# Expert input features regrouped so that each transposing product reads 128 neighbouring columns

## Chip, cores and metric

One core of one Trainium2 chip. The metric is device time in microseconds of one launch; lower is better.

## What is computed

One decoder layer on 512 tokens of 1024 features, in float32: RMSNorm, one projection, three token mixers (a state space model, a pooling, a block-sparse attention), an output projection and a residual, then a mixture of experts, and a last RMSNorm. The change touches only the input side of the experts:

```python
h = rms_norm(x, norm2_g[l])
# hier_moe: top-1 of 4 groups, then top-2 of its 4 experts; comb holds the weights
hg = jnp.einsum('td,edf->tef', t, w_gate)     # 16 experts, d = 1024, f = 256
hu = jnp.einsum('td,edf->tef', t, w_up)
act = jax.nn.silu(hg) * hu * comb[..., None]
y = jnp.einsum('tef,efd->td', act, w_down)
```

The sum over d may be taken in any order of the features, as long as a token's row and the rows of `w_gate` and `w_up` use the same one.

## The kernel before

The kernel is one stream of instructions per engine. A planner (`Flow`, lines 104 to 278) runs many small generators (`s_...`), estimates when each step could start, and so fixes the order in which every engine gets its instructions; on the chip each engine then works through its own list in that order and waits on semaphores. All instructions of the planner's part carry line 96, so groups of the profile are told apart by tile names.

The mixture of experts works on slots, not on tokens. Each of the 16 experts has 96 slots (`CAPACITY`), so 1536 slots, cut into 12 units of 128 slots. Routing (`s_route`, once for each of four blocks of 128 tokens, m = 0 to 3) computes logits (`pl`, from the transposed rows `h2T`), finds the two best experts (`hot`), counts places with a product against a triangle (`pc`), and gets each token's slot (`slot_i`). Then a token's scaled row (`xs_m[m]`: tiles `xp` for m = 0 to 2, tile `xs` for m = 3) goes two ways:

- Unit 0 does not go through memory. `s_gather` (lines 1414 to 1430) multiplies the rows of block m by a 0/1 matrix `sel` (128 tokens by 128 slots) and adds up over the four blocks in two PSUM banks `gb`. A block takes eight products, k = 0 to 7, each with 128 of the 1024 features as the stationary operand (loaded into the array by a weight load) and `sel` as the moving one. Products of float32 leave two records each in the trace, so a block shows 16 and all four 64.
- Units 1 to 11 are written to a scratch tensor by scatters (GpSimd, indirect DMA), read back (`xr`, one load per unit, issued by SyncE in `s_xt`), and transposed on TensorE in `unit_xt` (lines 1595 to 1606): eight transposes into `tx` per unit, again with 128 features of each row as the stationary operand and the identity (`cpk`) moving. One record each, 88 in all.

In both, product k reads the features k, k+8, k+16, ...: the row is seen as `(c k)`, so neighbouring columns of the stationary operand lie 8 float32 apart. This fits how the experts' first matrices are loaded: `source` (line 1618) puts rows 8p to 8p+7 of a matrix in partition p, as one stretch of memory, so that the k-th row of every partition is again k, k+8, ...

After the gather or the transposes, ScalarE casts to float16 (`xts`, the high part), VectorE makes the low part, and `s_gate_up` runs the unit's products `pg` (24 steps), then `s_down` the activation, two transposes `pta` and the products `py`. Expert weights stream through five staging tiles (`st_lde`), and each is split into two float16 parts by ScalarE and VectorE (`gu`, `dn`). A branch for the case that an expert gets more than 96 tokens (`tc.If(rv > CAP)`, line 1907) has its own copy of the expert code in float32, with a third use of `(c k)` at line 1923.

Of the kernel before, what the change touches and what calls it, by code (L numbers as in the profile page):

```python
# [19 lines left out]
P = 128  # L20
D = 1024
S = 512
KD = D // P
# [15 lines left out]
NE = 16  # L39
FE = 256  # L40
# [240 lines left out]
def hybrid_trunk_kernel(tc, a, out, cap=CAPACITY, dbg=None):  # L281
# [22 lines left out]
    v, act, pe, pool, sp = fl.v, fl.act, fl.pe, fl.pool, fl.sp  # L304
# [36 lines left out]
    ident = cpk[:, C_ID:C_ID + P]  # L341
# [23 lines left out]
    def bank(tag, name):  # L365
        return psum[HALF[tag]].tile([P, 512], F32, tag=tag, name=name, bufs=BANKS[tag])
# [888 lines left out]
    def s_route(m):  # L1255
# [96 lines left out]
        for i, (e, _, _) in enumerate(owners(0)):  # L1352
            if i == 0:
                v.tensor_scalar(sel, cpk[:, C_COL:C_COL + P], pl_c[:, e:e + 1], None, ALU.is_equal)
            else:
                v.scalar_tensor_tensor(sel, cpk[:, C_COL:C_COL + P], pl_c[:, e:e + 1], sel, ALU.is_equal, ALU.add)
        fl.sig(("sel", m))
        fl.spawn(1, s_gather(m))
        if m == NT - 1:
            fl.spawn(0, s_count())  # L1360
# [23 lines left out]
    xs_m = {}  # L1384
# [12 lines left out]
    def parts_out(u, h, ps, end):  # L1397

        yield "act"
        hi, lo = (xT_[u][:, i * KD + 4 * h:i * KD + 4 * h + 4, :] for i in range(2))  # L1400
        src = ps.rearrange("p (k n) -> p k n", k=4)
        act.copy(hi, src)
        yield "dve"
        v.tensor_tensor(lo, src, hi, ALU.subtract)
        end()

    def unit_end(u, h, tag, left):
        def end():
            fl.give(tag)
            left[0] -= 1  # L1410
            if not left[0]:
                fl.sig(("xT", u))
        return end

    def s_gather(m):

        yield "pe", ((("sel", m - 1), ("gather", 0, m - 1)) if m else (("wo_end", 1),)) + (("xs", m),), () if m else ("mm", "mm")
        if m == 0:
            M["gb"] = [bank("mm", f"gb{i}") for i in range(2)]
        src = xs_m[m].rearrange("p (c k) -> p k c", k=KD)  # L1420
        for k in range(KD):
            if k == 4:
                yield "pe"
            pe.matmul(M["gb"][k // 4][:, (k % 4) * P:(k % 4 + 1) * P], src[:, k], M["sel"][:, m, 0],
                      start=(m == 0 and k % 4 == 0), stop=(m == NT - 1 and k % 4 == 3))
        fl.sig(("gather", 0, m))
        if m == NT - 1:
            xT_[0] = xts[0]
            left = [2]
            for h in range(2):  # L1430
                fl.spawn(0, parts_out(0, h, M["gb"][h], unit_end(0, h, "mm", left)))

    def unit_in(u):
        return xts[u % NXT]
# [159 lines left out]

    def unit_xt(u, xr):
        left = [2]
        src = xr.rearrange("p (c k) -> p k c", k=KD)
        for h in range(2):
            yield "pe", ("B", ("xr", u)), ("tx1",) if h else ("tx0", "xT")
            if h == 0:  # L1600
                xT_[u] = unit_in(u)
            tx = psum[h].tile([P, 512], F32, tag=f"tx{h}", name=f"tx{u}_{h}")
            for k in range(4):
                pe.transpose(tx[:, k * P:(k + 1) * P], src[:, 4 * h + k], ident)
            fl.spawn(0, parts_out(u, h, tx, unit_end(u, h, f"tx{h}", left)))
        fl.give("xr")
# [287 lines left out]
    v, act, pe, pool, sp = nc.vector, nc.scalar, nc.tensor, nc.gpsimd, nc.sync  # L1894

    def rstd(pl, src, name, junk):
        ss = pl.tile([P, 1], F32, name="ss" + name)
        act.activation(junk, src, AF.Square, accum_out=ss)
        ms = pl.tile([P, 1], F32, name="ms" + name)
        pool.tensor_scalar(ms, ss, 1.0 / D, EPS, ALU.mult, ALU.add)  # L1900
        rs = pl.tile([P, 1], F32, name="rs" + name)
        pool.tensor_tensor(rs, ms, nhalf, ALU.pow)
        return rs
# [3 lines left out]
    with tc.If(rv > CAP):  # L1907
        with tc.tile_pool(name="fb", bufs=1) as fb, tc.tile_pool(name="psF", bufs=2, space=PSUM) as psF:
            sp.dma_start(cov_scr, cov)
            gff = fb.tile([P, D], F32, name="gff")  # L1910
            sp.dma_start(gff, a["final_norm_g"].to_broadcast([P, D]))
            g2f = fb.tile([P, D], F32, name="g2f")
            sp.dma_start(g2f, a["norm2_g"].to_broadcast([P, D]))
            xtf = [fb.tile([P, D], F32, name=f"xtf{t}") for t in range(NT)]
            hTf = fb.tile([P, KD, S], F32, name="hTf")
            hs = fb.tile([P, D], F32, name="hs")
            for t in range(NT):
                sp.dma_start(xtf[t], x2_scr[t * P:(t + 1) * P, :])
                rs = rstd(fb, xtf[t], f"h{t}", hs.bitcast(F16)[:, 0:D])
                v.scalar_tensor_tensor(hs, xtf[t], rs, g2f, ALU.mult, ALU.mult)  # L1920
                for k in range(KD):
                    pt = psF.tile([P, 512], F32, tag="pf", name=f"pf{t}_{k}")
                    pe.transpose(pt[:, 0:P], hs.rearrange("p (c k) -> p k c", k=KD)[:, k], ident)
                    v.tensor_copy(hTf[:, k, t * P:(t + 1) * P], pt[:, 0:P])
            for t in range(NT):
                for i in range(2):
                    yf = fb.tile([P, D], F32, tag="yf", name=f"yf{t}_{i}")
                    sp.dma_start(yf, y_scr[i * S + t * P:i * S + (t + 1) * P, :])
                    v.tensor_tensor(xtf[t], xtf[t], yf, ALU.add)
            wgf = fb.tile([P, 2, KD, FE], F32, name="wgf")  # L1930
            wdf = fb.tile([P, 2, D], F32, name="wdf")
            cvf = fb.tile([P, NT], F32, name="cvf")
            sgf = fb.tile([P, S], F32, name="sgf")
            aTf = fb.tile([P, 2, S], F32, name="aTf")
            with tc.For_i(0, NE, 1) as ei:
                for i, nm in enumerate(("moe_w_gate", "moe_w_up")):
                    sp.dma_start(wgf[:, i], a[nm][bass.ds(ei, 1)].rearrange("o (p k) f -> p (o k) f", p=P))
                sp.dma_start(wdf, a["moe_w_down"][bass.ds(ei, 1)].rearrange("o (k p) n -> p (o k) n", p=P))
                sp.dma_start(cvf, cov_scr[:, bass.ds(ei, 1), :].rearrange("p o t -> p (o t)"))
                for f in range(2):  # L1940
                    pgs = []
                    for i in range(2):
                        pg = psF.tile([P, 512], F32, tag=f"pg{i}", name=f"pgf{f}_{i}")
                        for k in range(KD):
                            pe.matmul(pg, wgf[:, i, k, f * P:(f + 1) * P], hTf[:, k, :],
                                      start=(k == 0), stop=(k == KD - 1))
                        pgs.append(pg)
                    act.activation(sgf, pgs[0], AF.Silu)
                    v.tensor_tensor(aTf[:, f, :], pgs[1], sgf, ALU.mult)
                for t in range(NT):  # L1950
                    for nh in range(2):
                        py = psF.tile([P, 512], F32, tag="pf", name=f"pyf{t}_{nh}")
                        for f in range(2):
                            pe.matmul(py, aTf[:, f, t * P:(t + 1) * P], wdf[:, f, nh * 512:(nh + 1) * 512],
                                      start=(f == 0), stop=(f == 1))
                        xs = xtf[t][:, nh * 512:(nh + 1) * 512]
                        v.scalar_tensor_tensor(xs, py, cvf[:, t:t + 1], xs, ALU.mult, ALU.add)
            for t in range(NT):
                rs = rstd(fb, xtf[t], f"z{t}", sgf.bitcast(F16))
                v.scalar_tensor_tensor(xtf[t], xtf[t], rs, gff, ALU.mult, ALU.mult)  # L1960
                sp.dma_start(out[t * P:(t + 1) * P, :], xtf[t])
# [11 lines left out]
def layouts(i, cap=CAPACITY):  # L1973

    f = {k: np.asarray(x) for k, x in i.items()}
    r = {"x": f["x"].reshape(S, D), "rel_bias": f["rel_bias"],
         "norm1_g": f["norm1_g"].reshape(1, D), "norm2_g": f["norm2_g"].reshape(1, D),
         "final_norm_g": f["final_norm_g"].reshape(1, D),
         "w_in": f["w_in"].reshape(D, NPROJ), "w_out": f["w_out"].reshape(D, D),
         "moe_w_gate": f["moe_w_gate"].reshape(NE, D, FE), "moe_w_up": f["moe_w_up"].reshape(NE, D, FE),  # L1980
         "moe_w_down": f["moe_w_down"].reshape(NE, FE, D)}

    def gpp(x):
# [17 lines left out]
    w = f["pool_w"].reshape(4, 64, 64)  # L2001
# [9 lines left out]
    c = np.zeros((P, C_W), np.float32)  # L2011
# [40 lines left out]
```

## Time and profile before

| what | us |
|---|---|
| median of 3 timed runs | 437.32 |
| the three runs | 436.31, 437.32, 441.03 |
| the profiled execution, whole | 435.2 |
| span of its instructions | 433.2 |
| mean granted TensorE clock in it | 0.951 of full speed |

All durations used below are of the profiled execution. Its time is 2.0 us more than the span, and 2.1 us under the median of the timed runs. PE is TensorE's products, PEld its weight loads (which may run beside products), DVE VectorE, ACT ScalarE, POOL GpSimd, SP SyncE, which issues most DMAs. In the timeline a row merges neighbouring instructions of one kind: its second number is from the first one's start to the last one's end, and "xN" is how many.

### The profile page before, as it was taken

Reading aid. Unit: us, or ns where it says so; the run is one execution under the profiler, and the core shown is the slowest. Engines: PE = TensorE matmul, PEld = TensorE weight load, DVE = VectorE, ACT = ScalarE, POOL = GpSimd, SP = SyncE. Lnnn points to the kernel's source line nnn. Section 1 sums busy time; section 2 is a strip of 40 time slices with the busy share of each in tenths; the row PEclk is TensorE's granted clock in tenths of the full one; section 3 lists DMA queues with packets and bytes.
Section 4 is the critical chain, followed back from the end, with each engine's and each line's share of the span. In section 5 each row is a group of like instructions: output and inputs, shape, how many; then the busy total and the mean of one; then the engine's idle time right before and its main releaser. Section 6 shows DMA issues by size and latency. Waiting matters only on the chain. (4 is left out here: it accounts for less than half of the span.)

```text
span 433.2 us, 8564 instructions
## 1 busy us (share of the span) xinstructions
PE 381.7 (88%) x3336; PEld 214.4 (49%) x3336; DVE 321.1 (74%) x650; ACT 236.3 (55%) x400; POOL 50.7 (12%) x86
## 2 busy tenths in 40 slices
PE   2899896898999999999999989899998876678992
PEld 1698453453644465445565975455454432233440
DVE  2798969747368778886898657978888777886383
ACT  4754133335469577865861115846786756466231
POOL 1200003124000000000124620001110010000011
PEclk9999999899999999999999978999998996589997
DMA  8935599219928979765786896548999996989933
GB/s 278 353 109 159 163 162 372 103 23 107 289 93 259 392 252 331 270 219 182 226 308 245 301 422 201 209 132 297 357 378 352 390 309 258 330 277 326 391 131 148
DMA packets 48872, 109.41 MB, mean 253 GB/s; under 512 B 4508, under 2 KB 25756, under 8 KB 48829
## 3 DMA queue, kind: packets, MB, share of 16 engines
q1 hardware_dynamic: 45676, 99.15, 70.0%
q0 software_dynamic: 2592, 9.44, 5.4%
q10 hardware_dynamic: 560, 0.25, 0.4%
q8 instruction: 27, 0.44, 0.4%
q14 instruction: 17, 0.13, 0.1%
HBM read 84.13 MB, written 24.69 MB: 251 GB/s over the span
## 5 line engine op out<-in xcount | busy, mean ns | idle before, releaser
L96 PE MATMUL pg<-gu,xts 128*32 128x512 f16 (+1 forms) x960 | 71.4, 397 | 6.6 <-ACT gu L96 6.6
L96 DVE SCALAR_TENSOR_TENSOR gu<-st_lde,gu 128x1024 f16<-128x1024 f32 x56 | 67.4, 1219 | 11.0 <-ACT gu L96 10.6
L96 ACT ACTIVATE gu<-st_lde 128x1024 f16<-128x1024 f32 x56 | 58.0, 1057 | 18.0 <-DMA st_lde<-in_moe_w_up_dram 10.3
L96 PEld LDWEIGHTS <-xts 128*32 128x32 f16 (+1 forms) x960 | 31.0, 103 | 42.3 <-issue 16.8
L96 PE MATMUL py<-dn,aT 128*32 128x512 f16 (+1 forms) x480 | 40.9, 443 | 6.6 <-ACT aT L96 5.8
L96 PE MATMUL px<-wo,cat 128*128 128x512 f16 x192 | 44.5, 379 | 0.0
L96 DVE SCALAR_TENSOR_TENSOR dn<-st_lde,dn 128x1024 f16<-128x1024 f32 x32 | 38.5, 1220 | 6.3 <-ACT dn L96 6.1
L96 ACT ACTIVATE dn<-st_lde 128x1024 f16<-128x1024 f32 x32 | 33.4, 1058 | 4.3 <-DMA st_lde<-in_moe_w_down_dram 4.2
L96 PEld LDWEIGHTS <-hT 128*64 128x64 f16 (+1 forms) x384 | 31.3, 156 | 5.3 <-issue 1.2
L96 ACT ACTIVATE pr<-pr,nm 128x128 f32<-128x128 f32 (+3 forms) x32 | 17.9, 559 | 22.3 <-DVE nm L96 22.3
L96 PEld LDWEIGHTS <-aT 128*32 128x32 f16 (+1 forms) x480 | 15.3, 109 | 28.6 <-issue 8.9
L96 PEld LDWEIGHTS <-cat 128*128 128x128 f16 x192 | 18.2, 98 | 22.3 <-issue 3.6
L96 DVE CUSTOM_DVE_ANT_0 pr<-psS,tb 128x128 f32<-128x128 f32 (+3 forms) x32 | 15.6, 486 | 14.8 <-PE psS L96 14.7
L96 PE MATMUL ps_v<-w_v,hT 128*128 128x256 f16 x192 | 24.8, 290 | 0.9 <-ACT hT L96 0.5
L96 POOL DMA_INDIRECT y_scr<-ys,tok x10 | 10.5, 1047 | 124.2 <-ACT ys L96 124.2
L96 PE MATMUL psS<-qk 64*64 64x128 f32 (+3 forms) x128 | 23.3, 451 | 0.7 <-ACT qk L96 0.7
L96 PE MATMUL ps_k<-hT,w_k 128*128 128x512 f16 x96 | 22.5, 380 | 0.0
L96 PE MATMUL ps_q<-hT,w_q 128*128 128x512 f16 x96 | 22.2, 380 | 0.0
L96 ACT COPY pts<-ptp 128x128 f32<-128x128 f32 (+3 forms) x32 | 13.1, 422 | 15.4 <-PE ptp L96 15.4
L96 PE MATMUL ptp<-cpk,pr 128*128 128x128 f32 x80 | 14.4, 285 | 7.8 <-DVE pr L96 7.8
L96 POOL TENSOR_TENSOR sm_r<-ss 128x1 f32<-128x1 f32 x4 | 3.6, 901 | 123.0 <-ACT xs L96 123.0
L96 ACT ACTIVATE ys<-py,cw 128x512 f32<-128x512 f32 (+1 forms) x14 | 9.6, 686 | 15.2 <-PE py L96 13.5
(240 smaller groups left out, 653.8 us busy)
## 6 DMA issues: line engine op xcount, KB each, us to landing
st_lde<-in_moe_w_down_dram SPq DMA_DIRECT2D x32, 512.0 KB
st_lde<-in_moe_w_gate_dram SPq DMA_DIRECT2D x28, 512.0 KB
st_lde<-in_moe_w_up_dram SPq DMA_DIRECT2D x28, 512.0 KB
x_scr<-zero SPq DMA_DIRECT2D x12, 512.0 KB
xr<-x_scr SPq DMA_DIRECT2D x10, 512.0 KB
xp<-in_x_dram SPq DMA_DIRECT2D x8, 512.0 KB
y_scr<-zero SPq DMA_DIRECT2D x8, 512.0 KB
yr<-y_scr SPq DMA_DIRECT2D x4, 1024.0 KB
```

What stands on the lines that cost most here:

```text
L96: r = f(*args, **kw)
```

## The change

A token's row is now seen as `(k c)`: product k reads the features 128k to 128k+127, which lie next to each other. So that the experts' first matrices still fit, the host reorders their rows before the launch: row 8p+k of the array handed to the kernel is feature 128k+p. The device's loads of these matrices, and all tiles, sizes and waits, are as they were.

```diff
@@ s_gather
-        src = xs_m[m].rearrange("p (c k) -> p k c", k=KD)
+        src = xs_m[m].rearrange("p (k c) -> p k c", k=KD)
         for k in range(KD):
...
             pe.matmul(M["gb"][k // 4][:, (k % 4) * P:(k % 4 + 1) * P], src[:, k], M["sel"][:, m, 0],
@@ unit_xt
-        src = xr.rearrange("p (c k) -> p k c", k=KD)
+        src = xr.rearrange("p (k c) -> p k c", k=KD)
@@ the branch for overfull experts
-                    pe.transpose(pt[:, 0:P], hs.rearrange("p (c k) -> p k c", k=KD)[:, k], ident)
+                    pe.transpose(pt[:, 0:P], hs.rearrange("p (k c) -> p k c", k=KD)[:, k], ident)
@@ layouts (host)
+    def spread(w):
+        return np.ascontiguousarray(w.reshape(NE, KD, P, FE).transpose(0, 2, 1, 3)).reshape(NE, D, FE)
...
-         "moe_w_gate": f["moe_w_gate"].reshape(NE, D, FE), "moe_w_up": f["moe_w_up"].reshape(NE, D, FE),
+         "moe_w_gate": spread(f["moe_w_gate"]), "moe_w_up": spread(f["moe_w_up"]),
```

In the planner's part every engine has the same instructions in the same order as before. Rows change places only in the branch for overfull experts, on VectorE, where an addition for the result (`yf` into `xtf`) stands four copies later:

```order
 L1924 COPY hTf<-pf_7_5171 128x128
 L1920 SCALAR_TENSOR_TENSOR hs<-xtf_5106,rsh_5179,g2f 128x1024
-L1929 TENSOR_TENSOR xtf_5105<-xtf_5105,yf_0_5244 128x1024
 L1924 COPY hTf<-pf_0_5182 128x128
 L1924 COPY hTf<-pf_1_5185 128x128
 L1924 COPY hTf<-pf_2_5188 128x128
 L1924 COPY hTf<-pf_3_5191 128x128
+L1929 TENSOR_TENSOR xtf_5105<-xtf_5105,yf_0_5244 128x1024
```

The addition moved behind four copies of a transposed block; the trace of before has no instruction of these lines, so the branch was not taken.

## Rows read from the trace of the kernel before

**Rows 1.** The page, parts 1 and 2: busy time of all engines, granted clock by slices.

```profile
PE 381.7 (88%) x3336; PEld 214.4 (49%) x3336; DVE 321.1 (74%) x650; ACT 236.3 (55%) x400; POOL 50.7 (12%) x86
PEclk9999999899999999999999978999998996589997
```

**Rows 2.** Busy time of each engine in seven stretches, with granted clock and DMA share.

```profile
core 0: us, PE busy (x) PEld busy (x) DVE busy (x) ACT busy (x) POOL busy (x), PEclk, DMA share, GB/s
248.00:251.00 3.00, 3.00 (x14) 3.00 (x14) 1.51 (x9) 0.00 (x0) 1.06 (x2) 0.50 1.03 415
255.00:258.00 3.00, 3.00 (x13) 3.00 (x14) 1.47 (x12) 0.81 (x2) 1.06 (x2) 0.50 1.03 421
258.10:264.30 6.20, 6.20 (x102) 3.27 (x101) 5.54 (x19) 2.49 (x3) 0.00 (x0) 1.00 0.75 277
264.30:267.50 3.20, 2.35 (x22) 2.04 (x25) 2.35 (x9) 2.13 (x4) 0.00 (x0) 1.00 0.27 92
268.30:271.60 3.30, 3.30 (x40) 1.16 (x28) 2.01 (x3) 1.01 (x2) 0.00 (x0) 0.50 0.98 338
271.90:329.80 57.90, 56.42 (x749) 29.69 (x746) 49.11 (x58) 42.18 (x59) 6.97 (x12) 1.00 0.78 280
329.80:385.40 55.60, 39.25 (x419) 17.96 (x417) 42.49 (x53) 35.83 (x47) 3.56 (x6) 0.81 0.90 319
```

**Rows 3.** Timeline of TensorE's products around the gather.

```profile
237.82 3.89 PE L96 MATMUL gb<-sel,xp 128*128 128x128 f32 x16
241.55 0.60 PE L96 MATMUL pth<-cpk,xp 128*128 128x128 f32 x4
...
242.35 2.16 PE L96 MATMUL gb<-sel,xp 128*128 128x128 f32 x8
244.35 1.86 PE L96 MATMUL pl<-rw,h2T 128*128 128x20 f32 x16
246.06 6.06 PE L96 MATMUL gb<-sel,xp 128*128 128x128 f32 x24
...
254.83 4.09 PE L96 MATMUL gb<-sel,xs 128*128 128x128 f32 x16 [2.11 <-DVE sel L96]
258.85 1.48 PE L96 MATMUL pg<-gu,xts 128*32 128x512 f16 x24
```

**Rows 4.** Timeline of VectorE in the same stretch, routing of the last blocks.

```profile
244.27 0.19 DVE L96 TENSOR_REDUCE sv__139<-sm_r 128x2 f32<-128x32 f32 x1
246.25 0.24 DVE L96 SCALAR_TENSOR_TENSOR sm_r<-pl,sm_r,rbias 128x20 f32<-128x20 f32 x1 [1.80 <-PE pl L96]
...
247.62 0.35 DVE L96 SCALAR_TENSOR_TENSOR sel<-cpk,sm_r,sel 128x128 f32<-128x128 f32 x1
...
249.49 0.23 DVE L96 TENSOR_SCALAR hot<-sm_r 128x16 f16<-128x16 f32 x1
252.58 0.17 DVE L96 TENSOR_TENSOR sm_r<-pc,cpk 128x16 f32<-128x16 f32 x1 [2.85 <-PE pc L96]
```

**Rows 5.** Weight loads grouped by form: busy us, mean ns of one, then idle before.

```profile
L96 PEld LDWEIGHTS gb<-sel,xp 128*128 128x128 f32 x48 | 11.8, 335 | 0.1
L96 PEld LDWEIGHTS tx<-cpk,xr 128*128 128x128 f32 x80 | 10.0, 194 | 5.8 <-issue 3.4 <-DVE xts L96 2.1 <-DVE dn L96 0.4
L96 PEld LDWEIGHTS pl<-rw,h2T 128*128 128x128 f32 x64 | 7.6, 192 | 0.1
L96 PEld LDWEIGHTS pth<-cpk,xp 128*128 128x128 f32 x32 | 3.9, 153 | 1.9 <-DVE xp L96 1.6 <-issue 0.2
```

**Rows 6.** Timeline of TensorE's products, two rows from later stages.

```profile
342.00 1.16 PE L96 MATMUL tx<-cpk,xr 128*128 128x128 f32 x8
...
418.02 2.74 PE L96 MATMUL pf<-yr,cpk 128*128 128x512 f32 x6
```

**Rows 7.** Timeline of POOL and SyncE's queue: last scatter, first read back.

```profile
255.13 0.95 POOL L96 DMA_INDIRECT x_scr<-xs,slot_i  x1 [0.19 <-issue]
...
266.28 0.36 SPq L96 DMA_DIRECT2D xp<-x_scr  x1
```

## The prediction

> **What bounds the kernel now.** I read the page first, then busy time by stretches, then the timelines of TensorE and VectorE around the gather, then the weight loads grouped by form. On the page TensorE is busy 88% of the span, VectorE 74%, and the granted clock dips in a slice near 250 us [rows 1]. The stretches say where TensorE sets the pace. From 271.90 to 329.80 it is busy 56.42 of 57.90 us at full clock; from 329.80 to 385.40 only 39.25 of 55.60, while the DMA share is 0.90, so there the stream of expert weights sets it [rows 2]. Ahead of both lies the passage from the output projection to the experts, some 20 us in which TensorE and VectorE take turns: gather of block 0, logits of block 3, gathers of blocks 1 and 2, places, gather of block 3, and only then the first gate and up product at 258.85 [rows 3]. Nothing of the expert stage can overtake that product, so a microsecond won there is a microsecond for all that follows, unless something later eats it.
>
> In this passage the gather is slow. 16 records of it take 3.89 us, or 0.243 each, where the 16 of the logits take 1.86, or 0.116, with the same 128 columns of float32 weights [rows 3]. The moving side can't be the reason: the products of 512 columns in the tail come at 2.74 / 6 = 0.457 us [rows 6], a quarter of which is 0.114 for the gather's 128 columns. The weight load differs: 335 ns for the gather, 192 for the logits [rows 5]. The logits read neighbouring columns, the gather every eighth. The gather keeps its 0.24 in a stretch at half clock too (24 records in 6.06 us, of which 248 to 251 ran at 0.50 [rows 2, 3]), as a load would that is longer than the product at either clock.
>
> **The change part by part.** No instruction, wait or byte of DMA is added or removed; the branch that reorders is not taken. Only the columns that 64 gather records and 88 transposes load become neighbours.
>
> The gather's new pace isn't in the trace. Its floor is the logits' 0.116, its ceiling the old 0.243 (worse than before is excluded, since the logits' load has the same shape and type). If load and product didn't overlap at all it would be 0.116 + 0.114 = 0.230; but the tail's products take 0.457 with a load beside each, so loads do hide. I take 0.116, the nearest row, at full clock. At half clock the product's 0.114 doubles to 0.228. A block of 16 then takes 1.86 us at full and 3.65 at half clock, against 3.89 to 4.09 now.
>
> A page speaks against any gain here. The Trainium skill, "TensorE: Matmul & The Clock Gate", section "LDWEIGHTS (loading the stationary operand)", gives a load's time by its number of columns alone; by it gather and logits would load alike and the change be worth nothing. The rows above don't agree: 335 against 192 ns with 128 columns in both. "Advanced Engine Details and Errata", "Memory Cachelines", would have it the other way, a penalty when each access goes to another 16-byte line, as 32-byte steps do. The gather's row agrees with that, the transposes' hardly.
>
> Now the passage, in order.
> - Block 0 ends 2.0 us earlier (3.89 to 1.86), and the eight records of block 1 that stand before the logits of block 3 save about another 1.2 (2.16 to 0.93). VectorE waits 1.80 us for these logits, after its row at 244.27 [rows 4]; that wait is all that can go, as the rest of its list up to there doesn't hang on the gather. So everything of VectorE from 246.25 on moves up 1.8: `sel` of block 2 is ready at 246.2 instead of 248.0, the last `hot` at 247.9 instead of 249.7.
> - TensorE now runs 24 gather records from 246.06 to 252.1 [rows 3], and the places of block 3 queue behind them; VectorE waits 2.85 us for these [rows 4]. After the change block 2 runs from 246.2 to 248.1 at full clock, to 249.9 at half. The places' product then needs only the last `hot`. VectorE's row at 252.58 thus moves up 4.0 us at full clock, 2.2 at half.
> - From that row to `sel` of block 3 VectorE works without a gap for 2.2 us, as before. Then the last gather: 4.09 us now, 1.86 at full clock (2.2 saved), 3.65 at half (0.4).
> - The first gate and up product so comes 6.2 us earlier if both gathers run at full clock, 2.6 if both at half. Before, both ran partly at 0.50 [rows 2], the first within 24 records in a row, the second after a wait of 2.11 us [rows 3], and I see no row by which to choose. I take the middle, 4.4.
> - The product behind them ran at full clock (1.00 from 258.10 to 264.30). A stretch at half clock as long as those in rows 2 would cost it half of 3.3 us, 1.65. I charge a quarter of that, 0.4.
>
> The transposes gain little. Their load takes 194 ns against 153 for neighbouring columns [rows 5], but eight take 1.16 us [rows 6] and four of the contiguous kind 0.60 [rows 3], 0.145 and 0.150 each, so the load is hidden behind the product before it except at the head of a group. 22 groups by the 41 ns are 0.9 us of TensorE; some five units lie in the stretch that it bounds, the others next to waits. I take 0.4; none at the low end, 88 x 41 ns = 3.6 us at the high one.
>
> What is late next: reading back unit 1. Its load (266.28 [rows 7]) waits in SyncE's queue behind weight loads, which wait for VectorE's splits, which come after the gather; so it moves up as well. It can't pass the scatters into the same tensor. The DMA share is 1.03 until 258.0, 0.75 until 264.3 and 0.27 after [rows 2], so the scatters had landed by 264.3 at the latest, 2 us before that issue. Their last issue (255.13) moves up 2 to 4 us too. I expect no new wait, or one under a microsecond. From 271.90 TensorE sets the pace and hands the shift on. The DMA-bound stretch after it starts its loads when experts are done, so it begins and ends earlier by the same.
>
> Sum: -4.4 + 0.4 - 0.4 = -4.4, on the profiled execution's 435.2: 430.8. The median of the timed runs lies 2.1 above that execution, so I give 432.9 for a median.
>
> **Rivals.** All times are medians.
> - *The clock takes the gain.* Shorter bursts with the same VectorE work between them leave TensorE slacker, so both gathers and the first expert products run at half clock. For it: both stretches at 0.50 in rows 2. Against it: at half clock the gather's array is busy nearly all the time, and it came back to 1.00 before the experts. -2.6 + 1.65 - 0.4 = -1.4: 436.0.
> - *Hidden anyway.* The weight stream is the true limit and starts no earlier; DMA share 0.90 from 329.80 on speaks for it. Against it, the share is 0.78 before, and loads wait there for tiles that experts free. A quarter of the shift is left, 1.1 us: 436.2.
> - *The row is misread*, and the pace of the gather comes from something other than the step between columns. Then nothing changes: 437.3. The equal shape of the logits' load speaks against it.
> - *All of it and more.* Both gathers at full clock, the transposes at twice my value: -6.2 - 0.8 = -7.0: 430.3.
> - *Slower: the read-back of unit 1 becomes the wait.* Weight loads that now issue 4 us earlier enter the queue while scatters drain at a share of 1.03. Each is 512 KB (128 partitions of 1024 float32), 1.2 us at 421 GB/s [rows 2]. From the point where the last scatter lands after about 266 us, unit 1 comes later than now, in spite of the earlier product. Three such loads in front give 264.3 + 3.7 = 268, 2 us late, then TensorE idles before it and runs 3.3 us at half clock, 1.65 more: +3.7, or 441.0. Against it: SyncE's list is in order, and only two weight loads stand ahead of the read-back.
>
> The Trainium skill, the same page on the clock gate, section "HAM oscillation — how this bites in real kernels", would also have the clock fall after waits between bursts; what it would do here is the first rival, and the half-clock rows after slack stretches agree with it.
>
> **How the numbers follow.** Forecast, as worked out, 0.58 (its own range 431.2 to 434.8, by the two clocks); more 0.18; clock 0.10; hidden 0.07; misread 0.03; slower 0.04. A measurement of this kernel tells about 1%, 4.4 us, from no change, and the forecast sits right on that line. Faster by over 1%: half of the forecast's cases, 0.29, and "more", 0.18, make 0.47. Slower by over 1%: 0.03, since the last rival's price sits near that line too. Within 1%: the other 0.50. The range leaves out the slower rival, part of the misread one and the far end of "more": 429.6 to 437.0.
>
> **What would show it.** In the profile after: weight loads of `gb` near 192 ns, 16 records in about 1.9 us, or 3.65 in a stretch at 0.50; VectorE's wait for the logits of block 3 gone, and that for the places of block 3 nearly so; the first `pg` at 252.7 to 256.3 instead of 258.85; `tx` loads near 153 ns and groups hardly shorter. Were `gb` still at 335 ns, the reading of the step is wrong. Were the first `pg` early and the end not, the weight stream hid it: then TensorE's idle time between 271.90 and 385.40 has grown by as much. Were the first `tx` no earlier, the scatters held it.

## The result, and the profile after

The changed kernel took 434.34 us (median of 12 runs), the kernel before 437.45 us (12 runs beside them). The ratio is 0.9918, 95% interval 0.9888 to 0.9947. A second set gave 434.03 us (7 runs) against 436.94 us (24 runs), ratio 0.9935, interval 0.9907 to 0.9963. So it is faster by 0.7 to 0.8%, about 3 us. That is less than 1%, inside the range, and smaller than the 4.4 us of the forecast (432.9). The prediction gave 0.50 to a change within 1% and 0.47 to a larger gain, so on which side of that line it fell was close to an even bet.

Some executions of both kernels are disturbed and take longer; the ratios leave them out, and as the first profiled execution of the changed kernel was one of them, the rows here are of the one taken in the second set (span 433.1 us).

That span is no shorter than the 433.2 us of before, and here is a first thing to learn. In it the first gather product starts at 240.13 us, against 237.82 before [rows 3]. Everything ahead of it is the same code. Single executions differ by more than the change is worth before the change is reached, so two spans say nothing; stretches that begin and end at the same instructions do.

The page, parts 1 and 2, answering to [rows 1]:

```profile
PE 376.4 (87%) x3336; PEld 208.1 (48%) x3336; DVE 321.1 (74%) x650; ACT 236.8 (55%) x400; POOL 52.9 (12%) x86
PEclk9999999699999999999999959999999896589997
```

TensorE is busy 5.3 us less and its weight loads 6.3 us less, with the same instructions. The dip of the granted clock near 250 us is deeper: 0.5, that is 1.2 instead of 2.4 GHz, for a whole slice.

The weight loads by form, answering to [rows 5] (busy us, mean ns of one):

```profile
L96 PEld LDWEIGHTS tx<-cpk,xr 128*128 128x128 f32 x80 | 8.7, 141 | 5.6 <-issue 3.8 <-DVE xts L96 1.9
L96 PEld LDWEIGHTS pl<-rw,h2T 128*128 128x128 f32 x64 | 7.5, 192 | 0.1
L96 PEld LDWEIGHTS gb<-sel,xp 128*128 128x128 f32 x48 | 7.4, 238 | 2.2 <-DVE sel L96 2.1
```

The transposes' loads fell from 194 to 141 ns as wanted. The gather's mean fell from 335 only to 238, not to the 192 of the logits. The timeline of TensorE's products, answering to [rows 3], shows why a mean is not enough here:

```profile
240.13 1.95 PE L96 MATMUL gb<-sel,xp 128*128 128x128 f32 x16
...
242.73 1.14 PE L96 MATMUL gb<-sel,xp 128*128 128x128 f32 x8
243.70 1.86 PE L96 MATMUL pl<-rw,h2T 128*128 128x20 f32 x16
245.41 1.14 PE L96 MATMUL gb<-sel,xp 128*128 128x128 f32 x8
248.45 3.78 PE L96 MATMUL gb<-sel,xp 128*128 128x128 f32 x16 [1.91 <-DVE sel L96]
252.16 0.19 PE L96 MATMUL pc<-base,one 1*128 1x16 f16 x1
...
254.98 3.78 PE L96 MATMUL gb<-sel,xs 128*128 128x128 f32 x16 [2.10 <-DVE sel L96]
258.69 6.42 PE L96 MATMUL pg<-gu,xts 128*32 128x512 f16 x96
...
271.67 1.06 PE L96 MATMUL tx<-cpk,xp 128*128 128x128 f32 x8 [0.49 <-DMA xp<-x_scr]
```

Two blocks run at the new pace (1.95 us for 16, and 1.14 for each half of block 1), two at 3.78 us. A load takes 192 ns (median) in blocks 0 and 1, and 333 ns in blocks 2 and 3; before it took 338 ns in block 0 already. The stretches, answering to [rows 2] (after the stretch: busy us of PE, PEld, DVE, ACT, POOL with their counts, then granted clock, DMA share, GB/s), show what tells them apart, the clock:

```profile
240.10:247.20 7.10, 6.45 (x60) 6.04 (x59) 5.71 (x21) 1.31 (x3) 3.89 (x8) 1.00 0.79 221
247.40:250.80 3.40, 2.35 (x11) 2.35 (x12) 2.57 (x15) 0.00 (x0) 2.85 (x6) 0.50 1.02 417
251.00:254.90 3.90, 1.88 (x23) 1.53 (x22) 1.90 (x11) 0.00 (x0) 0.88 (x1) 0.50 1.02 419
255.00:258.60 3.60, 3.60 (x16) 3.46 (x16) 2.24 (x14) 0.81 (x2) 1.16 (x3) 0.50 1.03 420
258.70:260.80 2.10, 2.10 (x23) 0.76 (x25) 1.67 (x5) 2.00 (x3) 0.00 (x0) 0.50 1.03 419
261.00:265.00 4.00, 4.00 (x80) 1.72 (x68) 3.90 (x15) 0.28 (x1) 0.00 (x0) 1.00 1.00 373
```

From 247.4 to 260.8 the clock is at half. A shorter gather left TensorE waiting for VectorE's selections, 1.91 and 2.10 us, and the clock fell around these waits. A wait is not the only thing that it falls with: in the kernel before it fell at 247.8 us, behind a stretch in which TensorE was busy throughout. That stretch of before:

```profile
237.60:247.80 10.20, 10.20 (x60) 10.01 (x59) 6.97 (x28) 1.31 (x3) 5.66 (x11) 1.00 0.82 271
```

VectorE's rows of the changed kernel, answering to [rows 4]:

```profile
246.69 0.23 DVE L96 SCALAR_TENSOR_TENSOR sm_r<-pl,sm_r,rbias 128x20 f32<-128x20 f32 x1
...
248.05 0.35 DVE L96 SCALAR_TENSOR_TENSOR sel<-cpk,sm_r,sel 128x128 f32<-128x128 f32 x1
...
249.98 0.23 DVE L96 TENSOR_SCALAR hot<-sm_r 128x16 f16<-128x16 f32 x1
252.72 0.17 DVE L96 TENSOR_TENSOR sm_r<-pc,cpk 128x16 f32<-128x16 f32 x1 [2.50 <-PE pc L96]
```

The wait of 1.80 us for the logits is gone; the wait for the places has shrunk only from 2.85 to 2.50, since the gather in front of them ran at half clock. From the first gather product to the first gate and up product the passage takes 258.69 - 240.13 = 18.6 us, where before it took 258.85 - 237.82 = 21.0. This is one execution, the slowest of its seven (435.09 us, median 434.03); two more profiles with the same gather, in the table below, have 17.4 and 18.2.

### The profile page after: what moved, and what is told of

It reads as the page before. It is cut to its first block, busy times and chain, and to the rows that moved or that the text cites. A ratio compares the mean times of both kernels' runs of the same rounds, so it can differ in the third digit from the quotient of the medians.

```text
span 435.6 us, 8564 instructions
## 1 busy us (share of the span) xinstructions
PE 378.5 (87%) x3336; PEld 209.5 (48%) x3336; DVE 321.2 (74%) x650; ACT 236.7 (54%) x400; POOL 53.4 (12%) x86
## 5 line engine op out<-in xcount | busy, mean ns | idle before, releaser
L96 PE MATMUL px<-wo,cat 128*128 128x512 f16 x192 | 47.4, 397 | 0.0
L96 PE MATMUL py<-dn,aT 128*32 128x512 f16 (+1 forms) x480 | 37.6, 409 | 6.1 <-ACT aT L96 5.4
L96 POOL DMA_INDIRECT y_scr<-ys,tok x10 | 13.0, 1297 | 118.9 <-ACT ys L96 108.0
L96 DVE CUSTOM_DVE_ANT_0 pr<-psS,tb 128x128 f32<-128x128 f32 (+3 forms) x32 | 15.6, 486 | 15.7 <-PE psS L96 15.7
L96 PEld LDWEIGHTS <-aT 128*32 128x32 f16 (+1 forms) x480 | 14.4, 103 | 26.1 <-ACT aT L96 7.5
L96 PE MATMUL psS<-qk 64*64 64x128 f32 (+3 forms) x128 | 23.6, 456 | 0.7 <-ACT qk L96 0.7
L96 ACT COPY pts<-ptp 128x128 f32<-128x128 f32 (+3 forms) x32 | 13.1, 422 | 16.3 <-PE ptp L96 16.3
L96 ACT ACTIVATE xs<-xp 128x512 f32<-128x512 f32 (+1 forms) x12 | 9.3, 772 | 15.1 <-DVE xp L96 11.4
```

The lines of the kernel that those rows point to most:

```text
L96: r = f(*args, **kw)
```

## The experiments

Theory: the step between columns makes the gather's loads long; the gather lies on the path, the transposes do not; and the clock takes back part of what the shorter gather gives. Rivals: the transposes carry it; the clock takes nearly all; the passage is set by VectorE alone.

This table gathers what the runs below showed. "Passage" runs from the first gather product to the first gate and up product, "then" from there to the first transpose of unit 1, both from one profile; ratios are to the kernel before, with intervals.

| kernel | passage | then | ratio |
|---|---|---|---|
| before | 21.0 | 13.0 | 1 |
| changed, second set | 18.6 | 13.0 | 0.9935 (0.9907 to 0.9963) |
| gather alone | 17.4 | 14.5 | 0.9940 (0.9908 to 0.9972) |
| transposes alone | 21.6 | 13.1 | 1.0021 (0.9993 to 1.0048) |
| changed, block 2 later | 16.1 | 13.8 | 0.9925 (0.9899 to 0.9951) |
| before, block 2 later | 20.4 | 13.0 | 0.9974 (0.9938 to 1.0010) |
| changed, second matrices | 18.2 | 13.6 | 0.9911 (0.9883 to 0.9940) |
| changed, idle products | 15.6 | 14.9 | 0.9881 (0.9839 to 0.9924) |
| the same again | 15.1 | 15.2 | 0.9871 (0.9821 to 0.9921) |
| the same, second matrices | 15.1 | 15.2 | 0.9853 (0.9792 to 0.9915) |
| before, idle products | 23.6 | 13.0 | 1.0055 (1.0021 to 1.0089) |

**The changed kernel again.**

> The changed kernel once more, for a profile to be read beside the one of before and a second interval. Theory (the step between columns makes the gather's weight load long, and the gather is on the path): ratio 0.988 to 0.994 against the kernel before; gather weight loads near 192 ns, the 16 records of a block in 1.9 us at full clock and about 3.5 us in a stretch at half clock; from the first gather product to the first gate and up product 18.0 us where before took 21.0 us. Rival (the clock takes most of it): the same stretch is 20 us or more whenever two gathers run at half clock, and the ratio is 0.995 to 1.0.

The ratio is 0.9935, at the theory's edge. The passage is 18.6 us, near the 18.0, with half clock in both late gathers. The rival's "20 us or more" did not come.

**The two halves apart.**

```diff
 # gather alone: s_gather only
-        src = xs_m[m].rearrange("p (c k) -> p k c", k=KD)
+        src = xs_m[m].rearrange("p (k c) -> p k c", k=KD)
 # transposes alone: unit_xt only
-        src = xr.rearrange("p (c k) -> p k c", k=KD)
+        src = xr.rearrange("p (k c) -> p k c", k=KD)
```

> Only the gather of unit 0 reads neighbouring columns; the transposes of units 1 to 11 still step by 8, and the experts' matrices keep their old order, so unit 0 pairs features with the wrong rows of its experts' matrices; no work is left out. Theory (nearly all comes from the gather): 0.75 to 1 of the whole change's gain, ratio 0.989 to 0.996. Rival (the 88 transposes carry it, since 88 loads lose 50 ns each, 4.4 us): ratio 0.997 to 1.003 here.

> Only the transposes of units 1 to 11 read neighbouring columns; the gather keeps its step of 8, and the experts' matrices their old order, so units 1 to 11 pair features with the wrong rows; no work is left out. Theory: transposes were hidden behind the product before them, so ratio 0.997 to 1.001 (0.4 us). Rival (the transposes carry the gain): ratio 0.989 to 0.994.

The gather alone gives 0.9940 (434.76 us, 12 runs), as much as the whole change in the second set. The transposes alone give 1.0021; their interval ends at 0.9993, so a gain of more than 0.3 us is excluded. The rival that they carry it is dead: their loads got 53 ns shorter each, and the time did not. TensorE's timeline in this run shows one thing more, a wait for the read-back of unit 1, on which a reading further down rests:

```profile
261.22 5.44 PE L96 MATMUL pg<-gu,xts 128*32 128x512 f16 x96
...
269.93 2.80 PE L96 MATMUL py<-dn,aT 128*32 128x512 f16 x48 [0.47 <-ACT aT L96]
274.30 1.06 PE L96 MATMUL tx<-cpk,xp 128*128 128x128 f32 x8 [1.56 <-DMA xp<-x_scr]
```

**Steps of 1, 2, 4 and 8.**

```diff
-        src = xs_m[m].rearrange("p (c k) -> p k c", k=KD)
+        d_ = (1, 2, 4, 8)[m]
+        src = xs_m[m].rearrange("p (b c d) -> p b d c", b=KD // d_, d=d_)
...
-            pe.matmul(..., src[:, k], M["sel"][:, m, 0],
+            pe.matmul(..., src[:, k // d_, k % d_], M["sel"][:, m, 0],
 # and the same in unit_xt with (1, 2, 4, 8)[u % 4]
```

> The kernel before with a step between columns of 1, 2, 4 and 8 float32 in the gather's four blocks, and the same steps in turn in the transposes of units 1 to 11 (step 2 in units 1, 5, 9; 4 in 2, 6, 10; 8 in 3, 7, 11; 1 in 4 and 8); features meet the wrong rows of the matrices, no work is left out. Read by single records. Theory as the memory lines of 16 bytes would have it: the gather's load is short (192 ns, 0.112 us between records) at steps 1 and 2, and long (335 ns, 0.240 us) at 8; step 4, where every column is on a new line, long as well. Rival (any step above 1 is slow): 2 is as long as 8. Rival (the length grows with the step): 4 lies between 2 and 8. Transposes: 140 ns at step 1, 193 at the others, 0.109 to 0.112 us between records at all steps.

TensorE's gather products in its timeline, blocks 0, 1 (in two halves), 2, 3 with steps 1, 2, 4, 8:

```profile
239.17 1.95 PE L96 MATMUL gb<-sel,xp 128*128 128x128 f32 x16
241.76 1.19 PE L96 MATMUL gb<-sel,xp 128*128 128x128 f32 x8
244.49 1.19 PE L96 MATMUL gb<-sel,xp 128*128 128x128 f32 x8
247.49 4.10 PE L96 MATMUL gb<-sel,xp 128*128 128x128 f32 x16 [1.81 <-DVE sel L96]
254.33 4.19 PE L96 MATMUL gb<-sel,xs 128*128 128x128 f32 x16 [2.09 <-DVE sel L96]
```

A step of 2 costs next to nothing (1.19 us for eight records, against 1.14 at step 1). A step of 8 doubles the time of a block at full clock (3.89 us before [rows 3], 1.95 here at step 1). Step 4 was measured at half clock only. There a block takes 3.78 us at step 1 (changed kernel), 4.10 at step 4 and 4.19 at step 8, so step 4 stands near step 8, but that it doubles the time at full clock is not shown. The Trainium skill, "Advanced Engine Details and Errata", "Memory Cachelines", has full speed as long as neighbours share a 16-byte line, which two of every four float32 do at step 2 and none at step 4. The trace agrees at steps 1, 2 and 8, and leans that way at 4.

The transposes follow another rule. Units 8 to 11, eight transposes each, steps 1, 2, 4, 8:

```profile
329.70 1.09 PE L96 MATMUL tx<-cpk,xr 128*128 128x128 f32 x8
340.89 1.23 PE L96 MATMUL tx<-cpk,xr 128*128 128x128 f32 x8
357.63 1.23 PE L96 MATMUL tx<-cpk,xr 128*128 128x128 f32 x8
378.21 1.16 PE L96 MATMUL tx<-cpk,xr 128*128 128x128 f32 x8
```

Every step costs a little, and 8 less than 2 or 4. That rule doesn't say so, and I have no cause for it.

**Where the gather stands.** The gather of block 2 is issued behind the places of block 3:

```diff
 # s_route, behind the products of pc
+        fl.sig(("pc", m))
 # s_gather, what it waits for
-    ... + (("xs", m),), ...
+    ... + (("xs", m),) + ((("pc", NT - 1),) if m == NT - 2 else ()), ...
```

> The changed kernel with the gather of block 2 issued on TensorE behind the places of block 3 instead of ahead of them; nothing else moves. Theory (after the change the gather of block 2 costs the path only what half clock adds to it, 3.7 instead of 1.9 us, and VectorE's 2.4 us wait for the places is this): VectorE's wait falls to about 0.6 us, the 16 records of block 2 run beside VectorE's 2.2 us of work on the last selection and stick out of it by up to 1.5 us at half clock; from the first gather product to the first gate and up product 17 us or a little more, ratio to the kernel before 0.987 to 0.993, 0.5 to 1.8 us below the changed kernel. Rival (VectorE's own list sets the passage, TensorE's wait is only seen there): no less than the changed kernel, 0.992 to 0.996.

> The same move of block 2's gather in the kernel before, with the step of 8 kept. Theory (a slow gather costs time only where VectorE waits for what stands behind it): the places of block 3 no longer wait for 16 records of 0.24 us, block 2 runs beside VectorE's selection and sticks out by 3.9 - 2.2 = 1.7 us, so about 1 to 2 us are won without any change of the step; ratio 0.994 to 0.999. Rival (only the load's length counts, not where the gather stands): 0.999 to 1.002.

In the changed kernel the passage falls to 16.1 us: VectorE no longer waits for the places behind a gather at half clock (0.26 us instead of 2.50). That is more than expected, because the last gather ran for the most part at full clock (2.24 us instead of 3.78). So VectorE's list alone doesn't set the passage, and the rival that it does falls. Yet the ratio is 0.9925, not to be told from the changed kernel's: what follows gives it back. TensorE now waits for the read-back of units 1 and 2, and unit 2's transposes start 34.1 us after the first gather product, against 33.6 in the changed kernel and 36.7 in before:

```profile
253.59 2.24 PE L96 MATMUL gb<-sel,xs 128*128 128x128 f32 x16
255.76 5.36 PE L96 MATMUL pg<-gu,xts 128*32 128x512 f16 x96
...
269.56 1.06 PE L96 MATMUL tx<-cpk,xp 128*128 128x128 f32 x8 [0.79 <-DMA xp<-x_scr]
273.75 1.23 PE L96 MATMUL tx<-cpk,xr 128*128 128x128 f32 x8 [3.13 <-DMA xr<-x_scr]
```

In the kernel before, VectorE's wait fell from 2.85 to 0.26 us too, but the passage only by 0.6: the moved gather takes 4.18 us and holds up the last one. The ratio 0.9974 has 1 in its interval, so this half stays open.

**Keeping the clock up.** Idle products of 128 columns, 26 ahead of the gather of block 2, 34 ahead of block 3's:

```diff
         if m == 0:
             M["gb"] = [bank("mm", f"gb{i}") for i in range(2)]
+            M["fill"] = bank("mm", "fill")
+        for i_ in range((0, 0, 26, 34)[m]):
+            nc.tensor.matmul(M["fill"][:, 0:P], tri16, one16, start=True, stop=True)
```

> The changed kernel with 26 idle products (128 columns of float16, into a PSUM bank that nothing reads) on TensorE ahead of the gather of block 2 and 34 ahead of that of block 3, where TensorE would wait for VectorE's selections; 1.5 and 1.9 us of work at full clock. Theory (the changed kernel loses 2 to 3 us in this passage to half clock, because TensorE is idle there): granted clock 1.00 in more of it, a block's 16 records nearer 1.9 us, first gather product to first gate and up product 15.5 to 17 us, ratio 0.984 to 0.991. Rival (the clock falls for another reason, or products into an unread bank only add work): the clock stays at 0.5 and the passage is as long or up to 2 us longer, ratio 0.992 to 1.0.

> The kernel before, step of 8 kept, with the same 26 and 34 idle products ahead of the gathers of blocks 2 and 3. Theory (with the long load a gather record takes 0.24 us at either clock, so a full clock is worth nothing to it): a block's 16 records stay at 3.9 to 4.1 us, the passage from the first gather product to the first gate and up product stays near 21 us or grows, ratio 0.998 to 1.005. The 26 stand ahead of block 2, whose selection is ready when TensorE arrives, so up to 1.5 us is added there. Rival (the clock is a cost of its own, in before as in the changed kernel): the passage shrinks by 1 us or more, ratio under 0.997.

In the changed kernel, timeline of TensorE's products:

```profile
245.34 1.61 PE L1422 MATMUL fill<-one,tri 128*128 128x128 f16 x26
247.41 2.05 PE L96 MATMUL gb<-sel,xp 128*128 128x128 f32 x16 [0.46 <-DVE sel L96]
...
249.92 2.29 PE L1422 MATMUL fill<-one,tri 128*128 128x128 f16 x34
252.72 2.05 PE L96 MATMUL gb<-sel,xs 128*128 128x128 f32 x16 [0.50 <-DVE sel L96]
254.70 5.36 PE L96 MATMUL pg<-gu,xts 128*32 128x512 f16 x96
```

Its passage as one stretch, clock 1.00 throughout:

```profile
239.00:254.60 15.60, 14.57 (x170) 13.71 (x168) 11.96 (x59) 2.11 (x5) 9.06 (x17) 1.00 0.89 323
```

Sixty products that compute nothing shorten the passage by 3.0 us (18.6 to 15.6; the later runs with them have 15.1). In the kernel before the same products lengthen it by 2.6 and the whole by 0.55%. Its timeline:

```profile
252.39 2.72 PE L1422 MATMUL fill<-one,tri 128*128 128x128 f16 x26
254.95 4.03 PE L96 MATMUL gb<-sel,xp 128*128 128x128 f32 x16
...
261.69 4.08 PE L96 MATMUL gb<-sel,xs 128*128 128x128 f32 x16 [0.20 <-DVE sel L96]
```

There the gathers of blocks 2 and 3 take 4.03 and 4.08 us, although the clock was 1.00 in both, where at half clock they took 4.09 to 4.19. So the pair tells the clock apart from the load: with the long load the clock is worth next to nothing to the gather, with the short one it is worth nearly half its time. The rival that the clock was a cost of its own falls.

**What holds the shorter passage.** SyncE's waits in the kernel with idle products, from 250 to 276 us (total, times, longest):

```profile
SPq L96 <- DVE vals L96: 11.5, 1, 11.5
SPq L96 <- DMA xr<-x_scr: 3.6, 1, 3.6
SPq L96 <- DMA x_scr<-xs,slot_i: 2.8, 1, 2.8
```

The third is the read-back of unit 1 waiting for the last scatter to land, a wait that the profiles of before and of the changed kernel shown here don't have. It grows as the passage shrinks: 0.2 us at a passage of 18.2 (second matrices), 1.1 at 17.4 (gather alone), 2.8 to 3.1 at 16.1 and below. The next run moves 2 MB of loads behind that read-back:

```diff
 # s_raw_loads; s_xt signals ("rb", u) when it has issued the load of unit u
-                yield "sp", (("wo_end", 1),), ("fly",)
+                yield "sp", (("wo_end", 1),) + ((("rb", NG),) if e == RAW[1] else ()), ("fly",)
```

> The changed kernel with the idle products, and the four loads of expert 6's first matrices (2 MB) issued behind the read-back of unit 1 instead of ahead of it. Theory (with the passage at 15.6 us the scatters land too late, and SyncE's 2.8 us wait for them before the read-back of unit 1 is the next bound; they share the DMA with these loads): the wait goes, the transposes of unit 1 start 13 us instead of 14.9 us after the first gate and up product, ratio to the kernel before 0.980 to 0.988. Rival (the scatters are slow by themselves, or expert 6's parts now come late): wait as before, or TensorE waits for expert 6's parts later; ratio 0.987 to 0.995.

The expectation came in part. SyncE's wait for the scatters fell from 2.8 to 1.8 us and did not go; unit 1 is transposed 264.88 - 255.23 = 9.7 us after the first gate and up product, even earlier than expected. The time is 0.9904 (0.9860 to 0.9949), no better. The planner had also put unit 1's transposes ahead of unit 0's last products and moved rows on other engines, so this run changed more than the one wait. That the wait costs time at the end is not shown.

**The second matrices.** The same regrouping for the two transposes `pta` of a unit:

```diff
-        acv = ac.rearrange("p (c k) -> p k c", k=2)
+        acv = ac.rearrange("p (k c) -> p k c", k=2)
 # and w_down's rows reordered on the host as (NE, 2, P, D) -> (NE, P, 2, D)
```

> The changed kernel with the same regrouping for the experts' second matrices: the two transposes pta of a unit read 128 neighbouring columns instead of every second one, and the host reorders the rows of these matrices to fit. Theory (a transpose's load is hidden behind the product before it, and its length matters only at the head of a group): pta loads fall from 202 to 140 ns, each unit's pair starts about 0.05 to 0.1 us earlier where TensorE waits for VectorE, under 1 us in all; ratio 0.990 to 0.995, not to be told from the changed kernel. Rival (each load is in the open, since the pair stands alone on TensorE): 24 x 0.06 = 1.5 us or more, ratio under 0.990.

> The changed kernel with the idle products once more, beside a second run of the kernel before. Theory (full clock in the passage is worth 2 to 3 us there, of which about 1 to 2 reach the end, since the scatters hold the read-back of unit 1): ratio 0.985 to 0.990, below the changed kernel's 0.9918 and 0.9935. Rival (the first run was luck): 0.991 to 0.995.

> Idle products and the regrouped second matrices together, the candidate for a version below both kernels. Theory: the two add, the second with under 1 us, ratio 0.983 to 0.989. Rival (the second gives nothing): the same ratio as with the idle products alone, within 0.003.

The `pta` loads fell from a mean of 205 to 141 ns; the ratio, 0.9911 (0.9883 to 0.9940), is the changed kernel's. The idle products gave 0.9871 (0.9821 to 0.9921) the second time, and with the second matrices 0.9853 (0.9792 to 0.9915). So the idle products held in both sets, 432.42 and 433.13 us, a version below both kernels by the middle of its intervals, though they overlap the changed kernel's. The four runs of the changed kernel with idle products have ratios of 0.985 to 0.990, the five with neighbouring columns in the gather and without idle products 0.991 to 0.994. What the second matrices add can't be told.

## Why the prediction was right, and where it was off

- **The weight load and the pace.** Right. 16 records take 1.95 us at full clock and 3.78 at half, against the predicted 1.86 and 3.65. The gather alone gives the gain. The number of columns alone does not set a load's time: 128 of them took 338 ns at step 8 and 192 at step 1, both at full clock.
- **VectorE's list.** Right. Its wait for the logits went, TensorE then waits 1.91 us for the selection of block 2, and the wait for the places remains as far as the gather ran at half clock.
- **The clock: the term that was mis-sized.** "I take the middle, 4.4" between 2.6 for two gathers at half clock and 6.2 for none. The profile shows both at half and 21.0 - 18.6 = 2.4; the gather alone, with part of block 2 at full clock, 3.6. The second matrices' run has 21.0 - 18.2 = 2.8. So the low end is the nearer one, as it is in the time: 434.34 lies near the slow end of the forecast's own range (431.2 to 434.8). The rows of before pointed to it: two half-clock stretches lay in the late gathers while they cost nothing [rows 2], and TensorE waited 2.11 us for VectorE ahead of the last one [rows 3]; a shorter gather was likely to add to such waits, and it added 1.91 us ahead of block 2. The idle products, which fill just these two waits, gave 5.4 to 5.9 (21.0 to 15.6 and 15.1), most of the 6.2.
- **The gate and up product.** Charged with 0.4 us; it lost 6.42 - 5.36 = 1.1 (5.36 is what it takes in the two faster passages above). But the path lost nothing: the way from the first gate and up product to unit 1's transposes is 13.0 us in both kernels, because these wait for the read-back of unit 1. In both it is issued 7.4 us after that product (266.28 - 258.85 [rows 3, 7], 266.13 - 258.69), and it lands some 5.6 us later. In the kernel before no wait shows, as `py` at half clock ended just then. With the transposes alone, `pg` and `py` ran at full clock (5.44 and 2.80 us), TensorE waited 1.56 us for the read-back, and the way was 13.1 us again. So in this profile the first rival had its condition, half clock in both gathers and into the first expert product; its charge of 1.65 us for that product is what failed.
- **The transposes.** 0.4 us forecast, nothing measured. Their loads were hidden, but not wholly: the prediction compared a group of eight with one of four, and eight at step 1 take 1.09 us instead of 1.16. Eleven units of 0.07 are 0.8 us of TensorE (an estimate), and none of it showed in the time.
- **The read-back of unit 1.** Right for this change: the read-back issues at the same distance as before and TensorE waits 0.49 us for it. "Under a microsecond" did not hold everywhere: with the gather alone TensorE waited 1.92 us for it, with the second matrices 2.27. The mechanism of the slower rival is real, though: SyncE's wait for the last scatter appears at a passage of 18.2 us and is 1.1 us at 17.4, and it takes back some of the faster passages.
- **Handing on.** Right. 2.4 to 3.6 us of passage, about 3 us in the time: what is won before the experts' first product is won at the end.

Sum as measured: about -3 us for the gather, 0 for the clock behind it and for the transposes, against -4.4. The sign, the place and the mechanism stood; the clock's share was too kind.

## What to carry to other kernels

Where the stationary operand of a float32 product steps through memory and the product is narrow, the weight load may be the pace; compare its ns with a load of the same shape that doesn't step, at the same granted clock (here a load without a step took 192 ns at full and 333 at half clock), and lay the data out on the host so that it doesn't. A faster step between two waits can drop the engine's clock and lose half of what it won; look at the granted clock around the waits before, even where it costs nothing yet. Shorter loads that were nearly hidden, as the 88 of the transposes were, can be worth nothing in the time.

## What the runs showed that I had not expected

Sixty products that nobody reads took 3 us off the passage, because they filled waits of about 2 us and the clock stayed at 1.00; with them the kernel came to 0.988 and 0.987 of the one before, without them to 0.992 and 0.9935, and these intervals overlap. A step of 2 float32 is nearly free for a gather's load (1.19 against 1.14 us for eight records). For a transpose a step of 8 is cheaper than one of 2 or 4 (1.16 against 1.23 us for eight), the other way round than for a product. Half clock in the first expert product cost the path nothing, as the read-back of unit 1 came later.
